# Where a pair's weighted sums stand: right behind the next pair's scores, in a projection bank, with two tiles for turned blocks

## The chip, the cores and the metric

The kernel runs on one core of a Trainium2 chip. The metric is the device time of one execution in microseconds; of the kernel before there are three runs, 392.85, 394.69 and 394.72 us (median 394.69). PE is TensorE (matmuls), PEld its loading of weights, DVE is VectorE, ACT is ScalarE, POOL is GpSimd, SP is SyncE, which here only issues DMAs.

## The reference

One decoder layer over x of 512 rows and 1024 columns, in float32:

```python
h = rms_norm(x, norm_w)
qa, ka, va, za, qb, kb, vb, zb, gl_a, gl_b = split(h @ w_in)       # 8 x 512 and 2 x 1024 columns
qa, ka = rms_norm(heads(qa), q_norm_w), rms_norm(heads(ka), k_norm_w)
oa = moba_attention(qa, ka, heads(va), rel_bias)     # 8 heads of 64: softmax(q k' + bias) v, causal
ob = stick_breaking_attention(heads(qb), heads(kb), heads(vb))     # 8 heads, weights from sigmoids
ya = (merge(oa) * silu(za)) @ w_up_moba
yb = (merge(ob) * silu(zb)) @ w_up_sb
y = sigmoid(gl_a + b1) * ya + sigmoid(gl_b + b2) * yb
out = x + y @ w_out
```

For 512 rows the block selection of the first attention keeps every earlier position, so both branches work on the lower triangle of 512 x 512 weights P for each head.

## The kernel before, in words

Every float32 product is made of three matmuls on a high and a low part (`mm3`, lines 171 to 175): weights arrive by DMA as `wr`, ACT copies the high part `wh` (L134) and DVE subtracts to get the low part `wl` (L136). Up to three weight tiles are made ahead (`load_w`).

**Opening.** Eight matmuls on a zeroed tile (`warm`, L167) fill the time until data lands. The projection of qa begins with `opening` (L200): four matmuls on `xh` of the first 128 rows of x' (made by DVE at L157), four on its low part, four with the low weights, and the same for the second slice. SP issues all loads: first half of `wr0`, the tile `x0` (small parameters and the first slice of x'), the second slice `xr`, second half of `wr0`, and so on.

**Projections by rows.** `section_tc` makes qa, ka, va and vb, each 96 matmuls in four PSUM banks. `GROUPS` says which of the eight banks: two have the tag `pj`, six the tag `s`. After qa, the row norms `r` are written to DRAM and read back over all partitions as `R`; `normalize` (L245 to L247) multiplies each slice of x' by it, reading `R` out of order through the view `Rt`, so that va and all later projections use normalised rows. qa and ka are normalised per head (L284 to L295), turned through DRAM and split.

**Pairs of heads.** Lines 593 to 613 go over eight pairs (four of branch a, four of branch b). For a pair, `scores` makes 24 matmuls with 64 rows each (L412, two heads side by side in the array) into six `s` banks. For each of its two heads, `softmax` (L422 to L426) or `stick` makes P on DVE and ACT, `turn` transposes 32 x 32 blocks into the tile `turned` (L454, one tile for all heads), `put` writes it to DRAM by four DMAs on SP (L460), and `get` reads it back as `pt` with one DMA on ACT's queue (L467). `weighted` (L479) multiplies the `pt` of both heads with v, two heads side by side in columns, and DVE multiplies the result with the gate (L483). `fill` puts projection work of 24 matmuls each between these steps; the table `FILLS` says which (names `za`, `zb`, `qb`, `kb`, `gl` and `ya` in the rows). A fill uses a `pj` bank, one of each pair an `s` bank.

In the kernel before, `finish(m - 1)`, which calls `weighted` for the pair before, stands behind the first two fills of pair m:

```python
        for b in range(2):
            if m and not b:
                finish(m - 1)
            if not b:
                done[m, 1] = get(*head(m, 1), done[m, 1])
```

The tail (`up`, `product`) makes the two up-projections and the output projection with sums of blocks. A scheduler lays the program out on each engine's queue from the order and priority of this text; DMAs that ACT issues stand in ACT's queue between its computations.

Of the kernel before, what the change touches and what calls it, by code (L numbers as in the profile page):

```python
# [9 lines left out]
F32 = mybir.dt.float32  # L10
F32R = mybir.dt.float32r
BF16 = mybir.dt.bfloat16
AF = mybir.ActivationFunctionType
ALU = mybir.AluOpType
AX = mybir.AxisListType

P = 128
S = 512
# [3 lines left out]
NT = S // P  # L22
# [5 lines left out]
BIG = 1e30  # L28
TW = S + P
SM = 32  # L30
WARM = 8
BLK = [0, 4, 7, 9, 10]
PQ = BLK[-1] * 32

# [4 lines left out]
BLOCKS = [b + h for b in ("11", "21", "12", "22") for h in "ab"]  # L39
OUT = [b + h for b in ("11", "21", "T2", "T1", "T3", "22", "T4") for h in "ab"]  # L40
# [17 lines left out]
def hybrid_layer(ctx: ExitStack, tc: tile.TileContext, x, xT, w, rel, out):  # L58
    nc = tc.nc
    V, A, G, T = nc.vector, nc.scalar, nc.gpsimd, nc.tensor  # L60
    PSUM = bass.MemoryType.PSUM

    cp = ctx.enter_context(tc.tile_pool(name="cp", bufs=1))
# [10 lines left out]
    def bank(tag, name):  # L74
        return pp.tile([P, S], F32, tag=tag, bufs=BANKS[tag], name=name)

    def slot(name, dt=F32):
        return gp.tile([P, S], dt, tag="g", name=name)


    warm = tp.tile([P, S], BF16, tag="sx", bufs=2, name="warm")
    V.memset(warm, 0.0)
    half = cp.tile([P, NT], F32, name="half")
    G.memset(half, -0.5)
    spare = cp.tile([P, NT], F32, name="spare")
    A.activation(spare, half, AF.Copy)
    x0 = cp.tile([P, SM + S], F32, name="x0")
    sm = x0[:, :SM]
    nw, mb, qw, kw = sm[:, 0:8], sm[:, 8:24], sm[:, 24:25], sm[:, 25:26]

# [25 lines left out]
    def fetch_w(c):  # L116
        cuts = ((0, 512), (512, 1024)) if c < 2 else ((0, 1024),)
        if c >= WO and OUT[c - WO][0] == "T":
            raw = sums[OUT[c - WO]]
        else:  # L120
            raw = wp.tile([P, 1024], F32, tag="wr", bufs=3, name=f"wr{c}")
            for a, b in cuts:
                if a == 0 and 0 < c < 4:
                    raw_x(2 * c)
                nc.sync.dma_start(raw[:, a:b], w[c if c < WO else WO + BLOCKS.index(OUT[c - WO])][:, a:b])
                if a == 0 and c < 4:
                    for k in (0, 1) if c == 0 else (2 * c + 1,):
                        raw_x(k)
        hi = wp.tile([P, 1024], F32R, tag="wh", name=f"wh{c}")
        lo = wp.tile([P, 1024], F32R, tag="wl", name=f"wl{c}")  # L130
        if c == 0:
            low[c] = load_x(0)
        for a, b in cuts:
            A.activation(hi[:, a:b], raw[:, a:b], AF.Copy)  # L134
            with tc.issue_after(low[0]) if c == 0 else nullcontext():
                low[c] = V.tensor_tensor(lo[:, a:b], raw[:, a:b], hi[:, a:b].bitcast(F32), op=ALU.subtract).ins  # L136
        return hi, lo
# [6 lines left out]
    def raw_x(k):  # L144
        if k == 0:
            xraw[k] = x0[:, SM:]
            nc.sync.dma_start(x0, xT[:, :SM + S])
        else:
            xraw[k] = slot(f"xr{k}")
            nc.sync.dma_start(xraw[k], xT[:, SM + k * S:SM + (k + 1) * S])  # L150

    def load_x(k):
        raw = xraw.pop(k)
        h = xp.tile([P, S], F32R, tag="xh", name=f"xh{k}")
        l = xp.tile([P, S], F32R, tag="xl", name=f"xl{k}")
        if k == 0:
            V.tensor_scalar(h, raw, nw[:, k:k + 1], None, op0=ALU.mult)  # L157
        else:
            A.activation(h, raw, AF.Copy, scale=nw[:, k:k + 1])
        last = V.scalar_tensor_tensor(l, raw, nw[:, k:k + 1], h.bitcast(F32), op0=ALU.mult, op1=ALU.subtract)  # L160
        xH.append(h)
        xL.append(l)
        return last.ins

    pw = bank("s", "pwarm")
    for i in range(WARM):
        T.matmul(pw, warm[:, :P], warm, start=True, stop=True)  # L167

    GROUPS = (("pj", "pj", "s", "s"), ("s", "s", "s", "s"))

    def mm3(ps, aH, aL, bH, bL, start, stop, on=False):

# [56 lines left out]
    r_dr = dp.tile([P, NT], F32, name="r_dr")  # L229

    nc.sync.dma_start(r_dr, r)
    nc.sync.dma_start(R, bass.AP(tensor=r_dr.tensor, offset=r_dr.offset, ap=[[0, P], [1, S]]))
    Rt = R.rearrange("q (p t) -> q t p", t=NT)

    again = {}

# [5 lines left out]
    def normalize(k):  # L242

        raw = again.pop(k)
        V.scalar_tensor_tensor(blocks(raw), blocks(raw), nw[:, k:k + 1], Rt, op0=ALU.mult, op1=ALU.mult)  # L245
        A.activation(xH[k], raw, AF.Copy)  # L246
        V.tensor_tensor(xL[k], raw, xH[k].bitcast(F32), op=ALU.subtract)  # L247

# [4 lines left out]
    oms = [cp.tile([P, n + 1], F32, name=f"om{n}{i}") for i, n in enumerate((P, 2 * P, S, S))]  # L253
    for om in oms:
        G.memset(om[:, om.shape[1] - 1:], 1.0)
    turned = cp.tile([P, 4, BLK[-1], 32], F32, name="turned")

    def take_v(ps, name):
        res = []
# [13 lines left out]
    def blocks(a):  # L273
        return a.rearrange("p (i t) -> p i t", t=P)
# [126 lines left out]
    def scores(br, p, q, k, res):  # L401

        (qh, ql), (kh, kl) = q[p], k[p]
        for grp in ((3,), (2,), (1, 0)):
            ps = [bank("s", f"s{br}{2 * p + b}{grp[0]}") for b in range(2)]
            c = 0
            for i in grp:
                n = (i + 1) * P
                for m, (x, y) in enumerate(((qh, kl), (ql, kh), (qh, kh))):
                    for b in range(2):  # L410
                        o = slice(b * HD, (b + 1) * HD)
                        T.matmul(ps[b][:, c:c + n], x[o, i * P:(i + 1) * P], y[o, :n], start=m == 0, stop=m == 2)  # L412
                for b in range(2):
                    res[2 * p + b][i] = ps[b][:, c:c + n]
                c += n
# [30 lines left out]


    def turn(br, h, rows):
        for i in (3, 2, 1, 0):
            for j in range(0, i + 1, 2):  # L450
                n = min(2, i + 1 - j)
                step = (BLK[j + 1] - 1 - BLK[j]) if n == 2 else 1
                at = BLK[j] + i - j
                V.transpose(turned[:, :, at:at + (n - 1) * step + 1:step, :].rearrange("p q j r -> p j q r"),  # L454
                            rows[i][:, j * P:(j + n) * P].rearrange("p (j q c) -> p j q c", j=n, q=4))

    def put(br, h):
        dr = dp.tile([P, 4 * PQ], F32, tag="pd", bufs=4, name=f"pd{br}{h}")
        for a in range(4):
            nc.sync.dma_start(bass.AP(tensor=dr.tensor, offset=dr.offset + a * PQ,  # L460
                                      ap=[[4 * PQ, 32], [32 * 4 * PQ, 4], [1, PQ]]),
                              turned[a * 32:(a + 1) * 32].rearrange("c q k r -> c q (k r)"))
        return dr

    def get(br, h, dr):
        pt = tp.tile([P, 4 * PQ], F32, tag="pt", bufs=5, name=f"pt{br}{h}")
        nc.scalar.dma_start(pt, dr)  # L467
        return pt

    ocol = {}  # L470

    def weighted(br, p, vv, pts):

        po = bank("s", f"po{br}{p}")
        for j in range(NT):
            for b in range(2):
                o, c = slice(b * HD, (b + 1) * HD), (2 * p + b) * HD
                src = pts[b].rearrange("p (a n) -> p a n", a=4)[:, :, BLK[j] * 32:BLK[j + 1] * 32]
                T.matmul(po[o, :].rearrange("p (a n) -> p a n", a=4)[:, :, j * 32:], vv[j][:, c:c + HD], src,  # L479
                         start=j == 0, stop=j == NT - 1, skip_group_check=True)  # L480
        ocol[br, p] = u = slot(f"o{br}{p}")
        dst, z = (by_block((mirror if br == "a" else blocks)(x)) for x in (u, zr[br, p]))
        V.tensor_tensor(dst, po.rearrange("p (a i r) -> p a i r", a=4, i=4).rearrange("p a i r -> p i a r"), z,  # L483
                        op=ALU.mult)
# [97 lines left out]
    done = {}  # L582
# [1 line left out]
    def head(m, b):  # L584
        return PAIRS[m][0], 2 * PAIRS[m][1] + b

    def finish(m):

        br, p = PAIRS[m]
        weighted(br, p, v_of[br], [done.pop((m, b)) for b in range(2)])  # L590
        split_o(br, p)

    for m, (br, p) in enumerate(PAIRS):
        q, k = (qa, ka) if br == "a" else (qb, kb)
        sc, rw = {h: [None] * NT for h in (2 * p, 2 * p + 1)}, {h: [None] * NT for h in (2 * p, 2 * p + 1)}
        scores(br, p, q, k, sc)
        for b in range(2):
            h = 2 * p + b
            bias = load_bias(h) if br == "a" else None
            (softmax if br == "a" else stick)(h, sc[h], rw[h], bias, (3, 2, 1, 0))  # L600
            turn(br, h, rw[h])
            done[m, b] = put(br, h)
            fill()
            if not b:
                done[m, 0] = get(*head(m, 0), done[m, 0])
        for b in range(2):
            if m and not b:
                finish(m - 1)
            if not b:
                done[m, 1] = get(*head(m, 1), done[m, 1])  # L610
            if (m, b) in SUMS:
                sum_w(SUMS[m, b], done[m, b])
            fill("pj" if b or not fills[1] and m < len(PAIRS) - 1 else "s")
# [168 lines left out]
```

## Time and profile before

| | before |
|---|---|
| runs, us | 392.85, 394.69, 394.72 |
| median, us | 394.69 |
| profiled execution, us (its span) | 392.84 (391.1) |
| PE busy | 385.3 us, 99% of the span |
| DVE, ACT, POOL busy | 69%, 51%, 14% |
| chain that ended last | PE 98%, DMA 1% |

The chain of waits says through which engine's work the end was reached; with 98% PE, time is won only where PE issues fewer or faster matmuls, changes between shapes less often, or begins earlier, and it is lost wherever PE is made to wait. 1.7 us of the profiled execution lie outside the span. In a timeline, a matmul's start is what to read: a 512-column matmul is shown with 0.39 us, but the next one starts 0.23 us after it.

### The profile page before, as it was taken

Reading aid. Unit: us, or ns where it says so; the run is one execution under the profiler, and the core shown is the slowest. Engines: PE = TensorE matmul, PEld = TensorE weight load, DVE = VectorE, ACT = ScalarE, POOL = GpSimd, SP = SyncE. Lnnn points to the kernel's source line nnn. Section 1 sums busy time; section 2 is a strip of 40 time slices with the busy share of each in tenths; the row PEclk is TensorE's granted clock in tenths of the full one; section 3 lists DMA queues with packets and bytes.
Section 4 is the critical chain, followed back from the end, with each engine's and each line's share of the span. In section 5 each row is a group of like instructions: output and inputs, shape, how many; then the busy total and the mean of one; then the engine's idle time right before and its main releaser. Section 6 shows DMA issues by size and latency. Waiting matters only on the chain.

```text
span 391.1 us, 5347 instructions
## 1 busy us (share of the span) xinstructions
PE 385.3 (99%) x1852; PEld 307.6 (79%) x1852; DVE 270.5 (69%) x534; ACT 199.1 (51%) x344; POOL 52.8 (14%) x100
## 2 busy tenths in 40 slices
PE   7999999999999999999999999999999999999996
PEld 4888888888887887887877887887887878888885
DVE  4823998855697576386498298489459524999962
ACT  4782523845779278393563372371354232359540
POOL 2018869000000000000000100010010000332110
PEclk9999999999999999999999999999999999999999
DMA  7978439982686865646546677576566642799835
GB/s 255 328 279 231 174 85 270 321 278 91 161 255 201 272 197 163 227 147 206 200 120 199 219 189 235 178 207 204 164 229 144 223 167 85 211 242 320 190 67 176
DMA packets 35946, 79.29 MB, mean 203 GB/s; under 512 B 3912, under 2 KB 16456, under 8 KB 35920
## 3 DMA queue, kind: packets, MB, share of 16 engines
q1 hardware_dynamic: 29584, 56.94, 45.3%
q0 software_dynamic: 2880, 9.44, 10.9%
q10 hardware_dynamic: 3456, 12.58, 9.8%
q8 instruction: 14, 0.23, 0.2%
q14 instruction: 12, 0.10, 0.1%
HBM read 62.15 MB, written 14.70 MB: 197 GB/s over the span
## 4 chain that ended last, share of the span: by engine, by line
PE 98%; DMA 1%; DVE 0%; SPq 0%; issue 0%
PE gl L173 8%; PE gl L174 7%; PE gl L175 7%; PE poa L479 2%; PE pob L479 2%; PE sb L412 2%; PE sa L412 2%; PE kb L173 2%; PE za L173 2%; PE zb L173 2%; PE qb L173 2%; PE va L173 2%; PE zb L174 2%; PE va L175 2%; PE ka L174 2%; PE yb L175 2%
## 5 line engine op out<-in xcount | busy, mean ns | idle before, releaser
L136 DVE TENSOR_TENSOR wl<-wr,wh 128x1024 fp32r<-128x1024 f32 (+1 forms) x64 | 76.1, 1189 | 49.8 <-ACT wh L134 49.2
L134 ACT ACTIVATE wh<-wr 128x1024 fp32r<-128x1024 f32 (+1 forms) x64 | 65.8, 1028 | 30.3 <-PE ya L175 11.4
L173 PE MATMUL gl<-xl,wh 128*128 128x512 f32 x128 | 50.9, 397 | 0.0
L174 PE MATMUL gl<-xh,wl 128*128 128x512 f32 x128 | 49.9, 390 | 0.0
L175 PE MATMUL gl<-xh,wh 128*128 128x512 f32 x128 | 49.8, 389 | 0.0
L505 ACT ACTIVATE gl<-gl,x 128x512 f32<-128x512 f32 x16 | 11.0, 689 | 34.9 <-PE gl L175 34.8
L173 PEld LDWEIGHTS gl<-xl,wh 128*128 128x128 f32 x128 | 24.0, 188 | 5.9 <-issue 0.9
L98 POOL COPY turn_of<-ptb 1x1 f32<-1x1 f32 x3 | 0.5, 175 | 206.1 <-DMA ptb<-pdb 206.1
L175 PEld LDWEIGHTS gl<-xh,wh 128*128 128x128 f32 x128 | 24.0, 188 | 5.0
L174 PEld LDWEIGHTS gl<-xh,wl 128*128 128x128 f32 x128 | 24.1, 188 | 4.6
L440 DVE TENSOR_TENSOR_SCAN sx<-om,begin 128x512 f32<-128x512 f32 (+3 forms) x32 | 24.8, 806 | 0.7 <-ACT om L436 0.7
L422 DVE CUSTOM_DVE_ANT_0 pa<-sa,om 128x512 f32<-128x512 f32 (+3 forms) x32 | 15.0, 477 | 10.9 <-PE sa L412 10.9
L424 ACT ACTIVATE pa<-pa,m 128x512 f32<-128x512 f32 (+3 forms) x32 | 17.9, 558 | 5.9 <-DVE m L422 5.6
L436 ACT ACTIVATE om<-sb 128x512 f32<-128x512 f32 (+3 forms) x32 | 14.6, 461 | 3.1 <-DVE sx L440 3.1
L454 DVE STREAM_TRANSPOSE turned<-pa 128x256 f32<-128x256 f32 (+1 forms) x48 | 15.2, 369 | 0.0
L454 DVE STREAM_TRANSPOSE turned<-pb 128x256 f32<-128x256 f32 (+1 forms) x48 | 15.0, 367 | 0.0
L438 ACT ACTIVATE pb<-sb 128x512 f32<-128x512 f32 (+3 forms) x32 | 14.8, 470 | 0.0
L442 DVE TENSOR_TENSOR pb<-pb,sx 128x512 f32<-128x512 f32 (+3 forms) x32 | 14.2, 474 | 0.1
L246 ACT ACTIVATE xh<-xs 128x512 fp32r<-128x512 f32 x8 | 5.0, 630 | 16.9 <-DVE xs L245 15.3
L173 PE MATMUL kb<-xl,wh 128*128 128x512 f32 x32 | 12.7, 396 | 0.0
L173 PE MATMUL zb<-xl,wh 128*128 128x512 f32 x32 | 12.7, 396 | 0.0
L173 PE MATMUL za<-xl,wh 128*128 128x512 f32 x32 | 12.7, 396 | 0.0
(305 smaller groups left out, 972.8 us busy)
## 6 DMA issues: line engine op xcount, KB each, us to landing
wr<-in_w SPq DMA_DIRECT2D x60, 512.0 KB, 4.3
pda<-turned SPq DMA_DIRECT2D x32, 160.0 KB, 3.1
pta<-pda ACTq DMA_DIRECT2D x8, 640.0 KB, 5.0
pdb<-turned SPq DMA_DIRECT2D x32, 160.0 KB, 3.0
ptb<-pdb ACTq DMA_DIRECT2D x8, 640.0 KB, 3.7
xn<-in_x SPq DMA_DIRECT2D x8, 256.0 KB, 5.7
xs<-in_xT SPq DMA_DIRECT2D x8, 256.0 KB, 6.7
om<-e_dr SPq DMA_DIRECT2D x8, 256.0 KB, 4.0
```

Source lines behind the costliest of these rows:

```text
L134: A.activation(hi[:, a:b], raw[:, a:b], AF.Copy)
L136: low[c] = V.tensor_tensor(lo[:, a:b], raw[:, a:b], hi[:, a:b].bitcast(F32), op=ALU.subtract).ins
L173: T.matmul(ps, aH, bL, start=start, stop=False, skip_group_check=on)
L174: T.matmul(ps, aL, bH, start=False, stop=False, skip_group_check=on)
L175: T.matmul(ps, aH, bH, start=False, stop=stop, skip_group_check=on)
L412: T.matmul(ps[b][:, c:c + n], x[o, i * P:(i + 1) * P], y[o, :n], start=m == 0, stop=m == 2)
L422: V.tensor_tensor_reduce(p, sc[i], bias[:, S - n:], scale=1.0, scalar=3e38, op0=ALU.add, op1=ALU.min, accum_out=m[:, 0:1])
L424: A.activation(p, p, AF.Exp, bias=m[:, 0:1], scale=-1.0, accum_out=m[:, 1:2])
L438: A.activation(p, z, AF.Sigmoid)
L440: V.tensor_tensor_scan(sx[:, n - 1::-1] if n == S else sx[:, :n][:, ::-1], om[:, e - n:][:, ::-1], begin[:, S - n:][:, ::-1], 0.0, op0=ALU ...
L454: V.transpose(turned[:, :, at:at + (n - 1) * step + 1:step, :].rearrange("p q j r -> p j q r"), rows[i][:, j * P:(j + n) * P].rearrange("p ...
L479: T.matmul(po[o, :].rearrange("p (a n) -> p a n", a=4)[:, :, j * 32:], vv[j][:, c:c + HD], src, start=j == 0, stop=j == NT - 1, skip_group ...
```

## The change

- `finish(m - 1)` now stands right behind `scores` of pair m, ahead of that pair's softmax and fills, and takes a `pj` bank instead of an `s` bank. The last pair's sums stay where they were.
- `turned` becomes a tile made anew for each head, from two buffers; the buffers for `pt` go from five to four.
- Nine warm-up matmuls instead of eight, on a tile of 128 columns read four times; their bank is `pj`, and qa, ka, va and vb take other banks.
- `x0` is loaded in two pieces and `xh` of it made in two, and the first half of `wr0` is issued by ACT instead of SP.
- `R` is loaded as `Rt` and copied by ACT into row order, so that `normalize` reads it straight.

```diff
-WARM = 8
+WARM = 9
...
-    warm = tp.tile([P, S], BF16, tag="sx", bufs=2, name="warm")
+    x0 = cp.tile([P, SM + S], F32, name="x0")
+    raw0 = wp.tile([P, 1024], F32, tag="wr", bufs=3, name="wr0")
+    nc.sync.dma_start(x0[:, :SM + P], xT[:, :SM + P])
+    nc.scalar.dma_start(raw0[:, :S], w[0][:, :S])
+    warm = tp.tile([P, P], BF16, tag="sx", bufs=2, name="warm")
...
-            nc.sync.dma_start(x0, xT[:, :SM + S])
+            nc.sync.dma_start(x0[:, SM + P:], xT[:, SM + P:SM + S])
...
-            V.tensor_scalar(h, raw, nw[:, k:k + 1], None, op0=ALU.mult)
+            for cs in (slice(0, P), slice(P, S)):
+                V.tensor_scalar(h[:, cs], raw[:, cs], nw[:, k:k + 1], None, op0=ALU.mult)
...
-    pw = bank("s", "pwarm")
+    pw = bank("pj", "pwarm")
...
-    GROUPS = (("pj", "pj", "s", "s"), ("s", "s", "s", "s"))
+    GROUPS = (("s", "s", "s", "s"), ("s", "s", "pj", "pj"))
...
-    nc.sync.dma_start(R, bass.AP(tensor=r_dr.tensor, offset=r_dr.offset, ap=[[0, P], [1, S]]))
-    Rt = R.rearrange("q (p t) -> q t p", t=NT)
+    Rt = slot("Rt")
+    nc.sync.dma_start(Rt, bass.AP(tensor=r_dr.tensor, offset=r_dr.offset, ap=[[0, P], [1, S]]))
+    A.activation(R.rearrange("q (t p) -> q t p", t=NT), Rt.rearrange("q (p t) -> q t p", t=NT), AF.Copy)
...
-        V.scalar_tensor_tensor(blocks(raw), blocks(raw), nw[:, k:k + 1], Rt, op0=ALU.mult, op1=ALU.mult)
+        V.scalar_tensor_tensor(raw, raw, nw[:, k:k + 1], R, op0=ALU.mult, op1=ALU.mult)
...
-    turned = cp.tile([P, 4, BLK[-1], 32], F32, name="turned")
...
     def turn(br, h, rows):
+        turned = tp.tile([P, 4, BLK[-1], 32], F32, tag="turned", bufs=2, name=f"turned{br}{h}")
...
-        pt = tp.tile([P, 4 * PQ], F32, tag="pt", bufs=5, name=f"pt{br}{h}")
+        pt = tp.tile([P, 4 * PQ], F32, tag="pt", bufs=4, name=f"pt{br}{h}")
...
-    def finish(m):
+    def finish(m, tag="s"):
...
         scores(br, p, q, k, sc)
+        if m:
+            finish(m - 1, "pj")
         for b in range(2):
             h = 2 * p + b
             bias = load_bias(h) if br == "a" else None
             (softmax if br == "a" else stick)(h, sc[h], rw[h], bias, (3, 2, 1, 0))
-            turn(br, h, rw[h])
-            done[m, b] = put(br, h)
+            done[m, b] = put(br, h, turn(br, h, rw[h]))
             fill()
...
         for b in range(2):
-            if m and not b:
-                finish(m - 1)
```

How this moves PE's queue at the second pair (`sa` are scores, `poa` the weighted sums of the first pair, `za` and `gl` fills). Before, the eight rows of `poa` stand together, two fills behind the scores:

```order
L173 MATMUL gl_1311<-xl_259,wh_1135 128x512
L174 MATMUL gl_1311<-xh_258,wl_1136 128x512
L175 MATMUL gl_1311<-xh_258,wh_1135 128x512
L479 MATMUL poa_1338<-pta_1059,vas_799 64x512
L479 MATMUL poa_1338<-pta_1131,vas_799 64x512
L479 MATMUL poa_1338<-pta_1059,vas_799 64x4x96
L479 MATMUL poa_1338<-pta_1131,vas_799 64x4x96
L479 MATMUL poa_1338<-pta_1059,vas_802 64x4x64
```

Now one row of `poa` stands behind the scores, and the other seven behind 15 matmuls of the fill `za`:

```order
L418 MATMUL sa_1190<-ka1h,qa1h 128x128
L487 MATMUL poa_1203<-pta_1064,vas_803 64x512
L179 MATMUL za_1261<-xl_112,wh_1105 128x512
...
L181 MATMUL za_1261<-xh_219,wh_1105 128x512
L487 MATMUL poa_1203<-pta_1137,vas_803 64x512
L487 MATMUL poa_1203<-pta_1064,vas_803 64x4x96
L487 MATMUL poa_1203<-pta_1137,vas_803 64x4x96
L487 MATMUL poa_1203<-pta_1064,vas_806 64x4x64
```

`pta_1064` and `pta_1137` are the blocks of the first pair's two heads. At the pairs three to eight all eight rows of `poa` or `pob` now stand together right behind the scores.

On ACT's queue, the DMA that fetches the first pair's second head stood, before, behind six exponentials of the second pair (the last two of them are of its second head):

```order
L424 ACT_TABLE_LOAD
L424 ACTIVATE pa_1198,m_1199<-pa_1198,m_1199 128x512
L424 ACTIVATE pa_1204,m_1205<-pa_1204,m_1205 128x384
L424 ACTIVATE pa_1210,m_1211<-pa_1210,m_1211 128x256
L424 ACTIVATE pa_1216,m_1217<-pa_1216,m_1217 128x128
L424 ACTIVATE pa_1270,m_1271<-pa_1270,m_1271 128x512
L424 ACTIVATE pa_1276,m_1277<-pa_1276,m_1277 128x384
L467 DMA pta_1131<-pda_1092 128x1280
```

Now it stands behind two of them:

```order
L430 ACT_TABLE_LOAD
L430 ACTIVATE pa_1219,m_1220<-pa_1219,m_1220 128x512
L430 ACTIVATE pa_1225,m_1226<-pa_1225,m_1226 128x384
L475 DMA pta_1137<-pda_1098 128x1280
L430 ACTIVATE pa_1231,m_1232<-pa_1231,m_1232 128x256
```

At the other pairs of branch a this DMA stood behind the next pair's first exponential or sigmoid; now it stands behind the reading and the weights of the third fill of its own pair, as at the pair of heads 4 and 5 (`gl_1649` is that fill):

```order
L513 ACTIVATE gl_1649<-gl_1624,x_78 128x512
L138 ACTIVATE wh_1653<-wr_1651 128x1024
L475 DMA pta_1616<-pda_1578 128x1280
L513 ACTIVATE gl_1682<-gl_1657,x_78 128x512
L138 ACTIVATE wh_1768<-wr_1766 128x1024
L430 ACT_TABLE_LOAD
```

## Rows read from the trace of the kernel before

**Rows 1.** The page: busy us (share of the span) and instructions of each engine.

```profile
PE 385.3 (99%) x1852; PEld 307.6 (79%) x1852; DVE 270.5 (69%) x534; ACT 199.1 (51%) x344; POOL 52.8 (14%) x100
```

**Rows 2.** Timeline of the opening: start us, us, engine line op [idle before <-releaser].

```profile
1.18 3.23 PE L167 MATMUL pwarm<-warm 128*128 128x512 bf16 x8 [1.18 <-DVE warm L82]
...
3.98 0.63 ACT L134 ACTIVATE wh<-wr 128x512 fp32r<-128x512 f32 x1 [1.76 <-DMA wr<-in_w]
...
4.64 0.49 DVE L157 TENSOR_SCALAR xh<-x 128x512 fp32r<-128x512 f32 x1 [3.52 <-DMA x<-in_xT]
...
5.28 1.16 PE L200 MATMUL qa<-wh,xh 128*128 128x512 f32 x4 [0.87 <-DVE xh L157]
...
6.97 0.72 ACT L159 ACTIVATE xh<-xr,x 128x512 fp32r<-128x512 f32 x1 [2.36 <-DMA xr<-in_xT]
...
7.60 0.61 ACT L134 ACTIVATE wh<-wr 128x512 fp32r<-128x512 f32 x1
...
8.27 0.76 PEld L200 LDWEIGHTS qa<-wh,xh 128*128 128x128 f32 x4 [0.41 <-ACT wh L134]
```

**Rows 3.** Stretches: us, busy (instructions) by engine, granted clock, DMA share, GB/s.

```profile
1.20:4.40 3.20, 3.20 (x8) 1.00 0.74 216
...
2.00:6.50 4.50, 3.63 (x12) 1.78 (x11) 1.82 (x3) 0.84 (x3) 0.61 (x2) 1.00 0.91 278
6.50:9.00 2.50, 2.50 (x11) 1.77 (x10) 1.29 (x3) 2.02 (x4) 0.00 (x0) 1.00 1.06 376
```

**Rows 4.** The chain that ended last, in order of time: start us, us, what.

```profile
49.37 0.36 PE va L173
...
111.66 2.07 PE sa L412 x24
113.73 0.43 PE za L173
114.16 0.23 PE za L174
...
124.82 2.30 PE poa L479 x16
...
138.22 2.07 PE sa L412 x24
```

**Rows 5.** Timeline of DVE: the last norm work ahead of va.

```profile
48.44 1.88 DVE L295 TENSOR_TENSOR qan<-qa,qast 128x512 f32<-128x512 f32 x3
```

**Rows 6.** Timelines of DVE and ACT: P of the first pair's second head, and its fetch.

```profile
106.70 0.29 DVE L426 TENSOR_SCALAR pa<-pa,m 128x128 f32<-128x128 f32 x1
...
114.68 0.55 DVE L422 CUSTOM_DVE_ANT_0 pa<-sa,om 128x384 f32<-128x384 f32 x1
...
119.10 0.33 ACTq L467 DMA_DIRECT2D pta<-pda  x1
```

**Rows 7.** DMA issues at 119, 192 and 181 us: count, KB, us to landing.

```profile
pta<-pda ACTq DMA_DIRECT2D x1, 640.0 KB, 5.2
...
pta<-pda ACTq DMA_DIRECT2D x1, 640.0 KB, 3.9
...
pta<-pda ACTq DMA_DIRECT2D x1, 640.0 KB, 6.8
```

**Rows 8.** Timeline of PE: out of the first scores, and into the first weighted sums.

```profile
94.74 0.28 PE L412 MATMUL sa<-ka0h,qa0l 64*128 64x128 f32 x2
94.85 0.27 PE L412 MATMUL sa<-ka0h,qa0h 64*128 64x128 f32 x2
95.06 0.50 PE L173 MATMUL za<-xl,wh 128*128 128x512 f32 x1
95.40 0.39 PE L174 MATMUL za<-xh,wl 128*128 128x512 f32 x1
...
124.43 0.39 PE L175 MATMUL gl<-xh,wh 128*128 128x512 f32 x1
124.75 2.37 PE L479 MATMUL poa<-pta,vas 128*64 128x512 f32 x16
```

More of the change, by code (lines that the diff above doesn't have):

```diff
@@ L86, in hybrid_layer @@
     A.activation(spare, half, AF.Copy)
-    x0 = cp.tile([P, SM + S], F32, name="x0")
     sm = x0[:, :SM]
@@ L120, in fetch_w @@
         else:
-            raw = wp.tile([P, 1024], F32, tag="wr", bufs=3, name=f"wr{c}")
+            raw = wp.tile([P, 1024], F32, tag="wr", bufs=3, name=f"wr{c}") if c else raw0
             for a, b in cuts:
@@ L124, in fetch_w @@
                     raw_x(2 * c)
-                nc.sync.dma_start(raw[:, a:b], w[c if c < WO else WO + BLOCKS.index(OUT[c - WO])][:, a:b])
+                if a or c:
+                    nc.sync.dma_start(raw[:, a:b], w[c if c < WO else WO + BLOCKS.index(OUT[c - WO])][:, a:b])
                 if a == 0 and c < 4:
@@ L163, in load_x @@
         return last.ins
-    pw = bank("s", "pwarm")
+    pw = bank("pj", "pwarm")
     for i in range(WARM):
-        T.matmul(pw, warm[:, :P], warm, start=True, stop=True)
-    GROUPS = (("pj", "pj", "s", "s"), ("s", "s", "s", "s"))
+        T.matmul(pw.rearrange("p (i t) -> p i t", t=P), warm, warm.unsqueeze(1).to_broadcast([P, NT, P]),
+                 start=True, stop=True)
+    GROUPS = (("s", "s", "s", "s"), ("s", "s", "pj", "pj"))
     def mm3(ps, aH, aL, bH, bL, start, stop, on=False):
@@ L455, in turn, with put @@
                             rows[i][:, j * P:(j + n) * P].rearrange("p (j q c) -> p j q c", j=n, q=4))
-    def put(br, h):
+        return turned
+    def put(br, h, turned):
         dr = dp.tile([P, 4 * PQ], F32, tag="pd", bufs=4, name=f"pd{br}{h}")
@@ L470, in hybrid_layer, with weighted @@
     ocol = {}
-    def weighted(br, p, vv, pts):
-        po = bank("s", f"po{br}{p}")
+    def weighted(tag, br, p, vv, pts):
+        po = bank(tag, f"po{br}{p}")
         for j in range(NT):
@@ L585, in head @@
         return PAIRS[m][0], 2 * PAIRS[m][1] + b
-    def finish(m):
+    def finish(m, tag="s"):
         br, p = PAIRS[m]
-        weighted(br, p, v_of[br], [done.pop((m, b)) for b in range(2)])
+        weighted(tag, br, p, v_of[br], [done.pop((m, b)) for b in range(2)])
         split_o(br, p)
```

## The prediction, made before the changed kernel ran

> **What bounds the kernel now.** The page comes first: PE is busy for 99% of the span [rows 1], so only PE's own queue can give or cost time. The chain of waits then shows what that queue is made of: from the opening to the tail it runs matmul behind matmul, each 0.23 us after the one before, and the exceptions are the first matmul behind scores or weighted sums, 0.43 us, and one of 0.36 us at the start of va [rows 4]. The timeline of the opening is where PE waits at all: 0.87 us ahead of the first real matmul, and a weight load at 8.27 us that waited for ACT [rows 2]. So three things can be won: a piece of the opening, the 0.13 us at va, and changes of shape. Everything else in the change matters only if it makes PE wait.
>
> **The opening.** The gate that counts is the later one. PE went on at 8.27 us because ACT made xh of the second slice from 6.97 us, when its DMA had landed, and the second half of wh from 7.60 to 8.21 us [rows 2]. Whatever the first matmul gains by landing earlier is waited for there, unless these two loads land earlier too. The same bytes stand ahead of them as before, x0 only in two pieces. The DMA engines moved 278 GB/s from 2.0 to 6.5 us at a share of 0.91, and 376 GB/s at 1.06 behind that [rows 3]. The ninth warm-up lengthens the warm-ups from 3.23 us to 9/8 of it, 3.63 us, so they end near 4.8 us; the first operands were there at 5.13 us (xh at 4.64 plus 0.49) [rows 2], so it hides in that wait, and costs what it overhangs if the data came much earlier. I take 0.1 us gained. At best all 24 opening matmuls run densely behind the warm-ups: 4.8 instead of 5.28 us, 0.5 us, and the later gate's wait of 0.41 us goes too, 0.9 us in all. At worst the two pieces land later and it costs 0.3 us. The share near 1 says that the engines, not the issuing queue, limit this stretch. The Trainium skill (DMA: Bandwidth & Descriptors, Issuing engines are not separate DMA queues) says that transfers issued by different engines run on the same 16 DMA engines and that a second issuer saves only issue time; by that rule the gain stays near my 0.1 us, while queues of their own would bring it near the 0.9 us. The trace so far, with its share of 0.91, agrees with the rule.
>
> **R, banks, buffers.** The 0.36 us at va is 0.13 us over the rhythm [rows 4]; the DVE work that ends just there is the last norm of qa, 48.44 to 50.3 us, whose first part frees the bank that va takes [rows 5]. With R in row order DVE's normalising is at most as long as before, and all of it stands ahead of that norm, so I count 0.13 us gained (0 to 0.13). The copy of R is one ACT instruction, hidden as ACT is busy for half the span [rows 1]. The new bank for weighted sums is wanted again one fill later (24 matmuls, 5.4 us), while DVE needs one instruction to empty it; four pt buffers hold two pairs, and only one pair's is open at a time. I cost all these at nothing; if the emptying came later than 5.4 us, the second fill of a pair would wait for it.
>
> **Six pairs where the sums move cleanly (pairs three to eight).** Leaving scores for a fill costs two things: the first fill matmul starts 0.21 us behind the last scores, which follow each other at 0.11, and its successor follows at 0.34 instead of 0.23, so 0.21 us together. Entering weighted sums from a fill takes 0.32 instead of 0.23 us, 0.09 [rows 8]. These two, 0.30 us, are replaced by one step from scores to weighted sums, which the trace never shows. If that step were free, a pair would gain 0.30 us; if it cost as much as both, 0. I take 0.10 us for it, the first half of what leaving scores costs, since the second half belongs to the fill's weight load. So 0.20 us a pair, 1.2 us in all (0 to 1.8). The Trainium skill (TensorEngine Tiling (Array Packing), Key Properties) says that changing the tiling mode drains TensorE, and scores (64*128) and sums (128*64) are two modes, so the step would not be free; by the rule the six give about my 1.2 us, without a drain there 1.8 us, and the sum below would be 0.6 us lower.
>
> **The second pair, where the sums are made to wait.** Here the order is different: one matmul row of the sums, 15 of the fill za, then seven rows, the first of which needs the second head of pair one. That head's fetch stands on ACT's queue behind the second exponential of pair two, which needs a DVE step that ended at 114.68 + 0.55 = 115.23 us [rows 6], in the middle of pair two's scores and softmax. Nothing in the change brings that step forward: it needs scores that end near 113.7 us [rows 4] and DVE's weight work ahead of it. The fetch at 119.10 came 0.2 us after its exponential began; so I put it at 115.4 us. P itself is no bound: its last DVE step ended at 107.0 us [rows 6], and with two turned tiles nothing holds the turning any more. The nearest fetch took 5.2 us to land, the quickest listed 3.9, the slowest 6.8 [rows 7]. I take 5.2, since it is the fetch of the same data with the same loads around it: landing at 120.6 us (119.3 to 122.2).
>
> On PE: scores end at 113.73 us. The first row is 512 of 1280 columns of a head and runs alone: 40% of 2.30 us, 0.92, to 114.65. Fifteen fill matmuls take 0.43 + 14 x 0.227 = 3.61, to 118.26 us. Then PE waits 2.3 us for the landing. Behind it stand the other head's first row alone, 0.92, the rest of both, 1.38, nine fill matmuls, 0.43 + 8 x 0.227 = 2.25, and three fills, 72 x 0.227 = 16.34: 20.89 us to the next scores. Before they began at 138.22 us [rows 4]. The loss is 120.6 + 20.89 - 138.22 = 3.3 us (2.0 to 4.9). Queued behind the waiting matmul is the whole fill; on DVE, the emptying of the sums stands in the softmax of the pair's second head and waits with them, so that head's turning comes about 2 to 3 us later, with the fetch of it 10 us away.
>
> At pairs three to five the fetch stands behind the third fill. The fourth fill (5.4 us) and the next scores (2.07) follow before the sums want it, 7.5 us, against 3.9 to 6.8 us to land: no wait, with 0.4 us to spare for the slowest. At the later pairs another fill lies between.
>
> **Sum.** +3.3 at the second pair, -1.2 for six steps, -0.13 at va, -0.1 at the opening: +1.9 us. On the profiled execution (392.84 us, span 391.1 and 1.7 around it) that gives 394.7 us. The runs shown have two levels, 392.85 and 394.7; the profiled one is at the lower, the median at the upper. I predict from the median: 394.69 + 1.9 = 396.6 us. This case's own range is 394.5 to 398.5 us, from wait and steps at either end.
>
> **Rivals.** *No wait: ACT's queue issues ahead.* If the fetch leaves before the exponential's input is there, it lands before 118.26 us and PE doesn't wait; that needs an issue before 118.26 - 5.2 = 113.1 us. Then the second pair only pays for its split sums, 118.26 + 20.89 - 138.22 = +0.9, and the whole is 0.9 - 1.4 = -0.5: 394.2 us, not slower. For it: P is ready long before. Against it: in the rows the fetch leaves after the start of the exponential ahead of it. *The wait repeats.* If the fetches of pairs three to five land like the slowest, or are asked for one fill later by a late put, each waits about a microsecond: +3, 399.6 us. For it: 6.8 us was measured in this very stretch; against it, 7.5 us of cover. *The clock falls in the wait.* The eight warm-up matmuls took 3.23 us, 0.40 each, which is 1.2 GHz for 512 columns, though the granted clock reads 1.00 there [rows 2, 3]; real ones follow at 0.23, which is 2.4 GHz. If the wait of 2.3 us sends PE back to that level for a stretch like the opening's, 3.23 us, half of it is lost: +1.6, 398.2 us. Against it: the idle 0.87 us at the opening was followed by full rhythm. The Trainium skill (TensorE: Matmul & The Clock Gate, Why this matters for your kernels) lists idle gaps between matmul bursts as what lowers the clock; no row here shows it in mid kernel.
>
> **How the numbers follow.** Forecast 0.62, no wait 0.16, repeated waits 0.12, clock 0.10. A measurement of this kernel tells about 0.5% (2.0 us) from no change. The forecast's +1.9 stands on that bound: I split its 0.62 into 0.27 slower and 0.35 same. No wait is same, 0.10, and, with the opening and the steps at their best, faster, 0.06. Both last cases are slower, but for 0.01: 0.21. Together slower 0.48, same 0.46, faster 0.06. The range 393.2 to 399.0 us leaves out the far ends of the no-wait and the repeated-wait cases and holds both levels of the runs.
>
> **What would show it.** Right: at the second pair one PE gap of 1 to 4 us ahead of the second row of poa, released by the DMA of pta, its fetch issued near 115.4 us; elsewhere scores run into sums with the chain's 0.43 us only behind the sums; the opening's gate still near 8.2 us; no piece of 0.36 us at va. Wrong: no gap there, a gap at each later pair, matmuls at 0.43 us behind the gap, or PE waits for a bank at a second fill.

## The result: slower by 1.0%, and the profile after

| | before | after |
|---|---|---|
| timed beside each other, median us (6 runs each) | 393.99 | 397.16 |
| least and most | 392.80, 394.88 | 396.56, 398.20 |
| profiled execution, us (its span) | 392.84 (391.1) | 397.19 (395.4) |

The ratio on record is 1.0098, 95% interval 1.0073 to 1.0122: slower. The two medians alone lie 3.2 us apart, the ratio makes it +3.9 us, the spans of the two profiles +4.3 us. The forecast was 396.6 us from a base of 394.69, so +1.9 us.

The page after, its line of busy times (answers to [rows 1]) and the line of the granted clock in 40 slices of the span:

```profile
PE 387.2 (98%) x1853; PEld 309.3 (78%) x1853; DVE 266.6 (67%) x535; ACT 192.1 (49%) x339; POOL 51.3 (13%) x100
...
PEclk9999999999998999999999999999999999999999
```

PE's share fell by a point with the same work but for one warm-up, so PE waits somewhere, and one slice, the thirteenth (118.6 to 128.5 us), has a lower clock. PE's waits (line, from whom, us in total, times, longest) name the place:

```profile
PE poa L487 <- DMA pta<-pda: 3.5, 1, 3.5
PE pwarm L172 <- DVE warm L86: 1.0, 1, 1.0
```

There is one wait behind the warm-up, and it is at the second pair. PE's timeline there (start us, us, what, [idle before, released by]):

```profile
112.92 0.27 PE L418 MATMUL sa<-ka1h,qa1h 64*128 64x128 f32 x2
113.12 1.07 PE L487 MATMUL poa<-pta,vas 128*64 128x512 f32 x2
114.13 0.50 PE L179 MATMUL za<-xl,wh 128*128 128x512 f32 x1
...
117.43 0.39 PE L181 MATMUL za<-xh,wh 128*128 128x512 f32 x1
121.31 3.83 PE L487 MATMUL poa<-pta,vas 128*64 128x512 f32 x14 [3.49 <-DMA pta<-pda]
125.08 0.50 PE L179 MATMUL za<-xl,wh 128*128 128x512 f32 x1
```

Two readings. The first sums of the second head stand 3.88 us behind the last fill matmul ahead of them, and their releaser is the DMA of `pta`. And the 14 sums behind the wait take 3.76 us from start to start of the next group, where all 16 took 2.30 before [rows 4]. The windows say why (stretch, us, busy by engine, granted clock, DMA share, GB/s):

```profile
113.00:117.50 4.50, 4.50 (x21) 2.98 (x19) 3.89 (x16) 3.80 (x9) 0.00 (x0) 1.00 0.95 304
117.50:121.30 3.80, 0.32 (x2) 0.00 (x0) 3.73 (x18) 1.41 (x4) 0.00 (x0) 0.95 0.80 295
121.30:123.50 2.20, 2.19 (x7) 1.19 (x9) 0.24 (x1) 0.60 (x2) 0.00 (x0) 0.50 0.75 176
123.50:125.10 1.60, 1.60 (x10) 0.87 (x6) 0.00 (x0) 0.00 (x0) 0.00 (x0) 0.75 0.54 172
125.10:127.20 2.10, 2.10 (x10) 1.75 (x10) 2.02 (x7) 1.27 (x4) 0.00 (x0) 1.00 0.00 0
```

The granted clock fell while PE idled; behind the landing it stood at 0.50, which is 1.2 GHz, and it was back at 1.00, 2.4 GHz, by 125.1 us. Next, why the landing was late. ACT's timeline (answers to [rows 6]) and the DMA issues from 112.3 to 119.5 us (count, KB, median us to landing; answers to [rows 7]):

```profile
114.47 0.72 ACT L430 ACTIVATE pa<-pa,m 128x512 f32<-128x512 f32 x1
114.98 0.33 ACTq L475 DMA_DIRECT2D pta<-pda  x1
...
115.19 0.60 ACT L430 ACTIVATE pa<-pa,m 128x384 f32<-128x384 f32 x1
```

```profile
wr<-in_w SPq DMA_DIRECT2D x2, 512.0 KB, 5.4
pta<-pda ACTq DMA_DIRECT2D x1, 640.0 KB, 6.3
om<-e_dr SPq DMA_DIRECT2D x1, 256.0 KB, 5.4
```

The fetch went out at 114.98 us, while the first of the two exponentials ahead of it still ran (114.47 to 115.19), and landed 6.3 us later, with two weight loads (issued at 112.5 and 114.3 us) and a load of biases around it. At the third pair, as at all later ones, nothing waits:

```profile
145.54 0.27 PE L418 MATMUL sa<-ka2h,qa2h 64*128 64x128 f32 x2
145.75 2.38 PE L487 MATMUL poa<-pta,vas 128*64 128x512 f32 x16
148.05 0.50 PE L179 MATMUL gl<-xl,wh 128*128 128x512 f32 x1
148.38 0.39 PE L180 MATMUL gl<-xh,wl 128*128 128x512 f32 x1
```

The sums start 0.20 us behind the last scores, take 2.30 us, and the wide step of 0.33 us (148.05 to 148.38) stands only behind the sums. From one pair's first scores to the next pair's, each of pairs three to eight is 0.19 us shorter (the eighth measured to its own last sums; six values of 0.192 to 0.195, 1.16 us together). The second pair takes 32.62 instead of 26.57 us. The opening (PE, PEld and ACT; answers to [rows 2]) lost its later gate:

```profile
4.86 1.43 PE L206 MATMUL qa<-wh,xh 128*128 128x512 f32 x4
5.33 0.53 PEld L206 LDWEIGHTS qa<-wh,xh 128*128 128x128 f32 x3 [0.28 <-DVE xh L162]
5.68 0.72 ACT L164 ACTIVATE xh<-xr,x 128x512 fp32r<-128x512 f32 x1 [0.87 <-DMA xr<-in_xT]
```

The second slice's `xh` begins at 5.68 and not 6.97 us; ka starts at 27.09 and not 27.45 us, and the first scores at 92.46 and not 92.99. So the profiles differ by -0.53 (up to the first scores) + 6.05 (second pair) - 1.16 (six pairs) = +4.36 us; the spans say +4.3.

### The profile page after: what moved, and what is told of

Its sections match the earlier page's. It is cut to its first block, busy times and chain, and to the rows that moved or that the text cites. A ratio compares the mean times of both kernels' runs of the same rounds, so it can differ in the third digit from the quotient of the medians.

```text
span 395.4 us, 5319 instructions
## 1 busy us (share of the span) xinstructions
PE 387.2 (98%) x1853; PEld 309.3 (78%) x1853; DVE 266.6 (67%) x535; ACT 192.1 (49%) x339; POOL 51.3 (13%) x100
## 4 chain that ended last, share of the span: by engine, by line
PE 96%; DMA 2%; ACT 1%; DVE 0%; issue 0%; ACTq 0%; DVEq 0%
PE gl L179 8%; PE gl L181 7%; PE gl L180 7%; PE poa L487 3%; PE pob L487 2%; PE sb L418 2%; PE kb L179 2%; PE zb L179 2%; PE zb L181 2%; PE kb L181 2%; PE yb L181 2%; PE yb L179 2%; PE vb L179 2%; PE va L181 2%; PE va L179 2%; PE ka L181 2%
## 5 line engine op out<-in xcount | busy, mean ns | idle before, releaser
L461 DVE STREAM_TRANSPOSE turneda<-pa 128x256 f32<-128x256 f32 (+1 forms) x48 | 16.4, 376 | 0.1
L461 DVE STREAM_TRANSPOSE turnedb<-pb 128x256 f32<-128x256 f32 (+1 forms) x48 | 15.9, 371 | 0.0
L487 PE MATMUL poa<-pta,vas 128*64 128x256 f32 (+3 forms) x64 | 12.0, 488 | 3.5 <-DMA pta<-pda 3.5
```

## Experiments

Where a kernel was run once, its span is given; the changed kernel's is 395.4 us.

**The first pair's sums put back.**

```diff
-        if m:
+        if m > 1:
             finish(m - 1, "pj")
 ...
+            if m == 1 and not b:
+                finish(m - 1)
             if not b:
                 done[m, 1] = get(*head(m, 1), done[m, 1])
```

> The first pair's sums alone are put back to their old place (behind two fills of the second pair, in a bank of the scores); all else is as in the changed kernel. Theory: the whole loss is the wait at the second pair (its period from scores to scores went from 26.57 to 32.62 us, +6.05), and the rest of the change gains 0.53 us ahead of the first scores and 0.19 us at each of six later pairs. Then this kernel's second pair takes 26.6 us again, no PE gap stands there, and it runs 1.7 us under the kernel before: a ratio of 0.9957, and 5.5 us or more under the changed kernel's span. Rival: the late fetch only moves its cost on (the fetches of the second pair stand behind it), and a wait of a microsecond or more shows at the third pair; then the ratio is 1.000 or above.

Measured: 391.26 us against 393.35 of before, ratio 0.9941 (0.9919 to 0.9963): faster than both kernels. The span is 389.5 us. The second pair takes 26.57 us, and behind the warm-up PE waits for nothing; the sums stand between two fills at full rhythm:

```profile
124.03 0.39 PE L181 MATMUL gl<-xh,wh 128*128 128x512 f32 x1
124.35 2.37 PE L487 MATMUL poa<-pta,vas 128*64 128x512 f32 x16
126.66 0.50 PE L179 MATMUL gl<-xl,wh 128*128 128x512 f32 x1
```

The whole loss was the second pair, and it isn't handed on. This is the version to keep.

**Zeros in the wait: is it the clock?** Three kernels add n matmuls of zeros to the fill's bank, between its fifteenth matmul and the sums that wait. Apart from them PE's order is the changed kernel's. The edit is cut to its main lines; `mid` holds the zeros and the sums behind them.

```diff
+            if k == 5 and mid:
+                mid.pop()(ps)
...
+                for _ in range(17):
+                    last = T.matmul(ps.rearrange("p (i t) -> p i t", t=P), zero,
+                                    zero.unsqueeze(1).to_broadcast([P, NT, P]), start=False, stop=False).ins
```

> The changed kernel with 17 matmuls of zeros, added to the fill's own bank, where PE waits 3.9 us for the second head (17 x 0.227 = 3.86 us); every other instruction of PE stands as it did. Theory: 1.5 of the 6.05 us lost at the second pair are the clock, which fell because PE idled: with PE kept busy the granted clock stays 1.00 behind the landing, the sums behind it follow each other at full rhythm (14 matmuls in about 2.0 us and not 3.8), the period is 31.2 and not 32.6 us, and the kernel runs 1.5 us under the changed one (395.6 beside 397.1). Rival: the slow rhythm belongs to the sums themselves, which read data that has only just landed; then the period stays 32.6 us and the 14 sums take 3.8 us as before.

> As the kernel with 17 matmuls of zeros, with 8: they cover 8 x 0.227 = 1.8 us of the wait and leave about 2.0 us, near the 2.3 us that the prediction gave the wait. If a wait of that size already brings the clock down, the sums behind it go at half rhythm (14 in 3.8 us) and the period stays 32.6 us; if the clock holds through it, the 14 sums take 2.0 us and the period is 31.2 us. The theory that the clock falls by idling allows both; the prediction's main case needs the second.

> The changed kernel with 5 matmuls of zeros in the wait: 1.1 us of it are covered and about 2.5 us of idle PE are left, the size that the prediction gave it (2.3). With 8 zeros and 1.6 us left the clock held. If the clock holds here too, the prediction's price of the wait was right for the wait it assumed, the period is 30.9 to 31.3 us, and the missing 1.5 us came only because the fetch landed later; if the 14 sums behind it take more than 2.4 us, the clock falls at the predicted size too, and the prediction's sum lacked it in any case.

With 17, 8 and 5 zeros the second pair took 31.27, 30.87 and 32.61 us; the kernel with 17 was timed at 396.08 us, ratio 1.0066 (1.0041 to 1.0090), 1.1 us under the changed kernel's 397.16 in another set of runs, and its span is 394.1 us (expected 1.5 under; 1.3 by the spans). The sums behind the wait and the window behind the landing, with 17 zeros:

```profile
121.49 2.37 PE L493 MATMUL poa<-pta,vas 128*64 128x512 f32 x14
...
121.30:123.50 2.20, 2.20 (x15) 1.25 (x14) 2.20 (x11) 1.03 (x4) 0.00 (x0) 1.00 0.71 159
```

with 8:

```profile
120.97 2.37 PE L493 MATMUL poa<-pta,vas 128*64 128x512 f32 x14 [1.48 <-DMA pta<-pda]
...
121.30:123.50 2.20, 2.20 (x15) 1.40 (x12) 1.89 (x10) 0.97 (x4) 0.00 (x0) 1.00 0.78 185
```

with 5:

```profile
121.05 3.96 PE L493 MATMUL poa<-pta,vas 128*64 128x512 f32 x14 [2.27 <-DMA pta<-pda]
...
121.30:123.50 2.20, 2.20 (x10) 1.20 (x9) 1.06 (x6) 0.91 (x4) 0.00 (x0) 0.50 0.81 195
```

Behind no wait and behind an idle 1.48 us the 14 sums take 2.30 us at clock 1.00, from their start to the next matmul's; behind 2.27 us idle they take 3.89 at 0.50, like the changed kernel's 3.76. So the slow sums are the clock, not their data. The runs beside the profiles say the same: the mean granted clock is 0.994 or 0.995 in all six of the changed kernel and 0.998 to 1.000 in all six with 17 zeros. A wait of the size that the prediction gave it, 2.3 us, cost the clock too, in the one execution that has such a wait. With 8 zeros the kernel is faster than with 5 by 1.7 us although it works more: those three matmuls bought the clock back.

The fall need not come inside the wait. In the kernel with one queue, further down, PE idled 3.34 us, the sums began at 122.13 us at 1.00, and the clock fell a good microsecond behind that:

```profile
122.10:123.30 1.20, 1.17 (x8) 0.75 (x10) 0.41 (x3) 0.60 (x2) 0.00 (x0) 1.00 0.50 116
123.40:126.80 3.40, 3.40 (x12) 1.99 (x9) 1.32 (x6) 0.59 (x2) 0.00 (x0) 0.50 0.54 147
```

The kernel with 17 zeros also prices the rest. From the last fill matmul ahead of the zeros (117.49 us) to the sums (121.49) pass 4.00 us, where a step from a fill into sums takes 0.32 [rows 8]: the zeros, which follow each other at 0.216 us, add 3.68. So the second pair without wait or slow clock takes 31.27 - 3.68 = 27.6 us, 1.0 us over before, the price of splitting the sums. In the changed kernel the same gap is 3.88 us, so the wait is 3.56, and the clock costs 1.47 (3.76 - 2.30, and 0.01 at the next fills): 1.0 + 3.56 + 1.47 is the 6.05 us lost, to 0.02.

**Two weight loads left out; the fetch on another queue.** The first kernel leaves out the loads issued at 112.5 and 114.3 us:

```diff
-        if c >= WO and OUT[c - WO][0] == "T":
+        if c in (21, 22):
+            raw = again["w"]
+        elif c >= WO and OUT[c - WO][0] == "T":
...
+        if c == 20:
+            again["w"] = raw
```

> The changed kernel without the two weight loads (512 KB each) that are issued at 112.5 and 114.3 us, just ahead of the fetch of the second head; the two fills that use them take the weights of the load before, so those gates are not computed with their own weights. PE, ACT and DVE keep their orders. Theory: the fetch took 6.3 and not 5.2 us to land since these loads share the DMA engines with it (316 GB/s from 115 to 121.3 us); without them it lands 1 to 2.5 us earlier, 3.8 to 5.2 us behind its issue, and the wait is 1.3 to 2.8 us. Rival: the fetch's own 640 KB in small rows set its time; then it lands 6 us or more behind its issue and the wait stays near 3.9 us.

The second changes the issuer of one fetch:

```diff
-        nc.scalar.dma_start(pt, dr)
+        (nc.gpsimd if br == "a" and h == 1 else nc.scalar).dma_start(pt, dr)
```

> The changed kernel with one edit: the fetch of the first pair's second head is issued by POOL, which has nothing to do there, and no longer by ACT behind the second exponential of the next pair. The four writes of that head's P land at 112.4 to about 113.7 us. Theory: ACT's queue holds the fetch about one microsecond (it went at 114.98 us); on POOL it goes right behind the last write, near 113.8 us, and with the 5.6 to 6.3 us that it needs among the weight loads lands near 119.6 us: the wait goes from 3.9 to about 2.5 us, not away, since P's own writes land too late. If the clock holds through such a wait the kernel runs 2.5 to 3 us under the changed one, otherwise 1.3 us. Rival: the exponential's place was all that held it; then the fetch goes well ahead of 113 us and lands before 118 us, and the wait is under half a microsecond.

Without the loads (issue, then PE):

```profile
pta<-pda ACTq DMA_DIRECT2D x1, 640.0 KB, 3.8
```

```profile
118.88 2.37 PE L491 MATMUL poa<-pta,vas 128*64 128x512 f32 x14 [1.00 <-DMA pta<-pda]
```

On POOL (issue, then PE):

```profile
113.49 0.83 POOL L475 DMA_DIRECT2D pta<-pda  x1 [48.43 <-DMA pda<-turneda]
```

```profile
121.13 3.89 PE L487 MATMUL poa<-pta,vas 128*64 128x512 f32 x14 [3.41 <-DMA pta<-pda]
```

Without the two loads the fetch landed 3.8 us behind its issue, the wait fell to 1.0 us, the clock held and the span is 391.0 us, 4.4 under the changed kernel, 4.0 of them at the second pair. So the loads in flight made the landing late.

On POOL the fetch left 1.5 us earlier, as the theory had it, but took 7.6 us and landed at 121.1 us. Its scores came 0.36 us later in that run, so half a microsecond of landing was gained, two fill matmuls fewer stood ahead of the sums, and PE idled as long as before (span 395.9): against my theory as much as against its rival. From 117.5 to 121.3 us that kernel moved 368 GB/s at a DMA share of 0.94. The same traffic may be what held the fetch, but POOL's fetch also goes by another queue (q0, `software_dynamic` on the page, where ACT's go by q10, `hardware_dynamic`), and no run tells the two apart. It couldn't have left earlier: by its profile POOL waited until 113.49 us for the writes of P to land, though their last one was issued at 108.55.

**One tile for turned blocks** (`bufs=1` for `turned`).

> The changed kernel with one tile for turned blocks of P in place of two. Theory: the second head's turning waits until the first head's four writes have read the tile, so P of the first pair's second head is written some 3 us later (from 110.4 us, as in the kernel before, and not from 106.8), its fetch goes out 3 us later or more, at 118 us or behind, and lands near 124 us; the sums wait until then unless more of the fill stands ahead of them, and the second pair costs 2 us more than in the changed kernel. At the later pairs the fetches have room (7 us) and nothing waits. Rival: the writes were never what the fetch waited for; then the second pair costs the same 6 us as in the changed kernel, within 0.5 us.

```profile
118.50 0.33 ACTq L475 DMA_DIRECT2D pta<-pda  x1
```

```profile
122.61 2.37 PE L487 MATMUL poa<-pta,vas 128*64 128x512 f32 x14 [1.68 <-DMA pta<-pda]
```

The writes of P left 3.0 us later and the fetch 3.5, as expected, but the second pair took 29.36 us, 3.3 less than in the changed kernel: the scheduler put 29 fill matmuls and not 15 ahead of the sums, PE idled 1.68 us and the clock held. My number was wrong by 5 us. In exchange pairs three to five now split their sums as well and take 1.61, 1.20 and 1.20 us more; the span is 396.3. So the second tile earns 4.0 us at those three pairs, where I had counted nothing for it, and at the second pair it goes with an order that has too little work ahead of the sums.

**The opening.** The first weights issued by SP, and the kernel before once more:

```diff
-    nc.scalar.dma_start(raw0[:, :S], w[0][:, :S])
+    nc.sync.dma_start(raw0[:, :S], w[0][:, :S])
```

> The changed kernel with the first half of the first weights issued by SP, behind the first piece of x, and no longer by ACT; all nine warm-ups stay. Theory: the opening gained since two queues issue side by side: with one queue every later load is issued 0.45 us later, ACT makes xh of the second slice at 6.1 us or later (5.68 in the changed kernel, 6.97 before), a gap stands at the fourth or fifth group of matmuls again, and ka starts 0.3 to 0.4 us later than in the changed kernel (27.4 and not 27.1 us). Rival: the smaller first piece of x was what helped, or the landing varies by itself; then xh comes within 0.3 us of 5.7 us and ka starts at 27.0 to 27.2 us.

> The kernel before once more, unchanged, for the spread of its opening. The runs of the changed kernel and of its variants with the same opening start ka at 27.02 to 27.70 us by themselves, and before was profiled once, at 27.45 us. Theory: the changed opening gains, and before starts ka at 27.4 us or later again. Rival: before varies as much, 27.1 to 27.7 us, and the 0.36 us between the two profiles is mostly chance.

The second slice's `xh` with one queue:

```profile
6.90 0.72 ACT L164 ACTIVATE xh<-xr,x 128x512 fp32r<-128x512 f32 x1 [1.50 <-DMA xr<-in_xT]
```

With one queue ka starts at 27.67 us, and `xh` of the second slice is back at 6.90 (span 396.4 us). Before again starts ka at 27.60. Ten profiles with the changed opening start it at 26.96 to 27.70, seven of them by 27.22, their median is 27.15; before has 27.45 and 27.60. So the changed opening gains about 0.4 us, with a spread as large.

Much of that spread goes with the clock. In two of the ten, both at 27.7, and in before again some of the first matmuls of qa follow each other at 0.43 us instead of 0.23, the rhythm of the warm-ups, which is 1.2 GHz for 512 columns. The trace's records of the granted clock begin at 4.2 to 5.1 us in the seven quick openings, at 5.76 in the one at 27.44, and at 6.78 and 6.89 in the two at 27.7. Before has 3.90, and yet 27.45, since its later gate still stood; before again has 6.27. Behind that first record no profile has the rhythm of 0.43 us any more. The 1.00 that a window shows ahead of its trace's first record, also the one of the warm-ups in [rows 3], is no reading: no record covers that time. Why the clock rose late in some executions stays open.

**The start of va.** R used as before (copy removed, the old strided read in `normalize`), and the old order of banks (`GROUPS` and the warm-ups' tag of before):

> The changed kernel with R used as before, read across its columns by the normalising instructions, without the copy into order of t. Theory: the piece of 0.36 us at the start of va, and its twin of 0.31 right behind, came from a bank that was freed late, since the norm of qa stood behind six normalising instructions that each took longer; with the old R the norm ends about 2 us later than in the changed kernel, and va's first two steps cost 0.13 us again. Rival: the new order of banks took them away; then va starts 0.227 us behind the last matmul of ka, as in the changed kernel, and nothing else on PE moves either.

> The changed kernel with the old order of banks: qa and the warm-ups, and with them va, in the banks they had before (two of the projections' and two of the scores' for qa and va). All engines keep their orders. With the old R the two wide steps at the start of va stayed away, so theory: the order of banks took them away, and here va starts 0.28 us or more behind ka's last matmul, with 0.1 to 0.2 us lost in all by the start of vb. Rival: it was the norm of qa, which now runs 2.5 us earlier on DVE (45.96 and not 48.44 us); then va starts at 0.227 us here too.

Both theories fell: va starts 0.226 and 0.227 us behind ka (spans 396.5 and 396.7 us; their second pairs took 33.1 and 33.4 us, with PE idle for 3.8 and 4.0 us, so the wait itself varies by half a microsecond). The kernel before, run again, shows the same without any change:

```profile
49.13 0.39 PE L175 MATMUL ka<-wh,xh 128*128 128x512 f32 x1
49.36 0.39 PE L173 MATMUL va<-wl,xh 128*128 128x512 f32 x1
```

So the 0.36 us of [rows 4] belonged to one execution. R in row order does make the eight normalising instructions shorter (781 instead of 1161 ns each), but PE waits for none of them.

## Why the prediction was right and where it was not

- **The wait at the second pair: right in place, mechanism and sign, too small.** It was put ahead of the second head's first sums, released by the DMA of `pta`, its fetch issued at 115.4 us; with the 0.53 us gained earlier that is 114.9, and it went at 114.98. The split was priced at 0.9 us and cost 1.0. The term that failed is the landing: 5.2 us were taken from the fetch of before [rows 7], with the words that the same loads stand around it. They do not: the fetch moved 4 us forward, to 2.5 and 0.7 us behind two weight loads that in before had been issued 6.2 and 4.3 us ahead of it. It took 6.3 us (3.8 without them), and the wait came to 3.56 and not 2.3 us. That P itself is no bound was read from DVE's last step, at 107.0 us; in the run with POOL its writes had landed only by 113.49, so about 1.5 us were to be had from an earlier issue, and the issue before 113.1 us that the rival of no wait needs was out of reach there.
- **The clock: a rival at 0.10 that came true.** I held against it that idling 0.87 us at the opening [rows 2] was followed by full rhythm. That row says nothing about longer waits, and in the run with 2.27 us idle a wait of the forecast's own size cost the clock: about 1.5 us that the sum put at nothing. The rival's +1.6 us came within 0.1 us of its price, in part by luck, since its 3.23 us were the length of eight warm-ups, a number that the program chose, and the 1.00 that it wondered at had no record behind it. The Trainium skill (TensorE: Matmul & The Clock Gate, Why this matters for your kernels) had idle gaps between bursts as the cause; the trace agrees, with 0.50 behind the gap.
- **Wait repeats, no wait: neither came.** The sixteen fetches took 3.9 to 7.8 us to land, and all but this one had work to cover them. An issue 1.5 us earlier, by POOL, did not take the wait away.
- **Six pairs: right.** 0.20 us each, 1.2 in all; measured 0.19 and 1.16. The new step from scores to sums costs 0.11 us, where I took 0.10. The Trainium skill (TensorEngine Tiling (Array Packing), Key Properties) says that a change of tiling mode drains TensorE; the trace agrees in that the step isn't free.
- **The opening: the wrong gate.** I wrote that the later gate stays near 8.2 us, since the same bytes stand ahead. It went, as `xh` of the second slice came 1.3 us earlier, though its load was issued at 1.62 us, where before it was at 1.63. The gain is about 0.4 us in place of 0.1. The rule I leaned on, the Trainium skill's (DMA: Bandwidth & Descriptors, Issuing engines are not separate DMA queues), speaks of saved issue time. The runs hint at more than that: `xh` of the second slice begins at 5.54 to 6.61 us in the ten openings with two queues (in the middle near 5.9), at 6.90 with one queue, whose load is issued 0.48 us later, and at 6.97 and 6.83 before, whose load is issued at the same time. With a single run of one queue and a spread of a microsecond among the ten, how much more is not shown, and what the second queue changes in the transfers stays open.
- **va: no effect of the change.** The profiles differ by 0.17 us up to vb, but before run again has no wide step there; one row of one execution was priced as if it came back each time.
- **Sum.** Forecast +3.3 - 1.2 - 0.13 - 0.1 = +1.9; the profiles +6.05 - 1.16 - 0.53 = +4.36, where the 6.05 are split 1.0, wait 3.56 and clock 1.47. The time fell close to the forecast since the runs beside it had before at 393.99, 0.7 us under the base that I used; the difference was twice what I forecast.

## What to carry to other kernels

A wait of TensorE can cost more than its length: price it once as idle time and once as what follows at the lower clock, and look whether a few more matmuls ahead of it keep the clock. When a DMA is moved, its landing time does not move with it: count the transfers that will be in flight at the new place. If one iteration of a loop has less work to cover a load than the others, leave that iteration in the old order and take the gain from the rest: with the first pair's sums put back, the rest of this change is 0.6% faster than before.

## What was not expected of the hardware

An idle time of 2.27 us was followed by a granted clock of 0.50 and 3.89 us for 14 sums; ones of 1.00, 1.48 and 1.68 us were followed by 1.00 and 2.30. With one queue the clock stayed at 1.00 through an idle time of 3.34 us and fell behind it, while PE worked. Ahead of a trace's first record of the clock a window shows 1.00 without a reading; there only the rhythm of the matmuls tells the level, 0.43 or 0.23 us for 512 columns. A 640 KB fetch from ACT landed 6.3 us behind its issue just behind two weight loads, and 3.8 us without them.
